# Seven products instead of eight for part of a gated unit's projections, in a two-layer decoder trunk

## The chip, the cores and the metric

The kernel runs on one core of one Trainium2 chip. The metric is the device time of one execution in microseconds (us). A core has five engines with a queue of their own each: TensorE (PE in the profile, with PEld for the loads of its stationary operand), VectorE (DVE), ScalarE (ACT), GpSimd (POOL) and SyncE (SP), which here only issues DMAs. Each engine takes its instructions in the order in which the program emits them; engines wait for each other by semaphores.

## The reference

Two decoder layers on 256 tokens of width 1024, all in float32. Each layer has four sub-layers between norms:

```python
h += 1/2 * post(SwiGLU_a(pre(h)))
h +=       post(W_out [ norm(MLA heads) ; norm(dilated-window heads) ])
h += 1/2 * post(SwiGLU_b(pre(h)))
h +=       post((p[i] W_ple) * sigmoid(pre(h) W_gate))

def swiglu(x, w_gate, w_up, w_down):
    return (jax.nn.silu(x @ w_gate) * (x @ w_up)) @ w_down
```

`x` is 256 x 1024, `w_gate` and `w_up` are 1024 x 2816 and `w_down` is 2816 x 1024. There are four such gated units (two per layer), and their weights are most of what is read and multiplied.

## The kernel before

**Precision.** A float32 number is split into two pieces of 12 significant bits, hi and lo, kept as fp32r. A product x @ w is three matmuls per block of 128 in the contracted dimension: hi.hi, hi.lo and lo.hi (`mm3`, lines 321 to 323). A matmul takes a 128 x 128 block of x, transposed, as stationary operand and up to 512 columns of w as moving operand.

**Weights.** `Weights` streams all weights in the order of use. A load on SP's queue brings a raw tile of 128 x 2048 float32 (1 MB, four buffers). `prepare()` makes one piece of 128 x 1024 out of half a raw tile: ACT copies it to hi (line 152), then DVE subtracts to get lo (line 153). Ten pairs of hi and lo are there in the gated units, eight in the attention, where the other two pairs' memory holds attention tiles (`kdt`, `grp`, `vm`, `vd`).

**A gated unit** (`ffn`) walks over six chunks of the hidden width: five of 512 columns and one of 256. The 256 tokens are two tiles, t = 0 and 1. Per chunk TensorE does gate for both tiles, up for both tiles (G0, G1, U0, U1; in a unit that follows another sub-layer the first chunk goes G0, U0, G1, U1), 24 matmuls each at 512 columns, and then down (D0, D1), also 24 each, into four PSUM banks that are kept over the whole unit. Between them ACT applies silu to gate (line 448), DVE multiplies it with up (`hm`, line 453), TensorE transposes that (`tp`, line 398), and ACT and DVE split the transpose into hi and lo (lines 401 and 402) as the stationary operand of down.

**Order.** The emission order is written out: `PLAN` lists, for each phase of matmuls, at which steps (three matmuls each) a weight piece is prepared and at which steps other work is inserted. A phase that finds a piece missing prepares it on the spot (`need`).

```python
self.nc.scalar.activation(hv, raw, AF.Copy)
self.nc.vector.tensor_tensor(lv, raw, hv.bitcast(F32), op=ALU.subtract)
...
gate(0, c, *(pend if c == 0 else []), lo_last=False)
gate(1, c)
hm0 = up(0, c)
hm1 = up(1, c, h0)
...
down(0, c, h1)
down(1, c)
```

`h0` and `h1` are the transposes and splits of the two tiles' products (`hid_t`); `pend` is what is left of the norm and the transposes of the sub-layer before.

Of the kernel before, what the change touches and what calls it, by code (L numbers as in the profile page):

```python
# [17 lines left out]
P = 128  # L18
D = 1024
# [17 lines left out]
NRAW = 4  # L37
CHUNKS = [(0, 512), (512, 512), (1024, 256), (1280, 512), (1792, 512), (2304, 512)]
# [58 lines left out]
class Weights:  # L97
# [3 lines left out]
    def __init__(self, nc, raw_pool, slots):  # L101
# [3 lines left out]
        self.shut = set()  # L105
        self.slot = {}
        self.specs = []
        self.loads = []
        self.raw = {}
        self.got = {}  # L110
        self.next = 0
        self.next_load = 0

    def add(self, keys, src, a, n):
        load = len(self.loads)
        self.loads.append((src, a * len(keys), n))
        for i, key in enumerate(keys):
            self.specs.append((key, load, i, a, n, i == len(keys) - 1))

    def load_one(self):  # L120
        i = self.next_load
        if i >= len(self.loads):
            return
        src, a, n = self.loads[i]
        raw = self.raw_pool.tile([P, 2048], F32, tag="raw", name=f"raw{i}")
        view = raw[:, : a * n].rearrange("p (a n) -> p a n", n=n)
        if i == 0:
            for j in range(0, a, a // 2):
                self.nc.sync.dma_start(view[:, j : j + a // 2], src[:, j : j + a // 2])
        else:  # L130
            self.nc.sync.dma_start(view, src)
        self.raw[i] = view
        self.next_load += 1

    def pick(self):
        return next((i for i in self.free if i not in self.shut), None)

    def can(self):
        return self.next < len(self.specs) and self.pick() is not None

    def prepare(self):
        key, load, part, a, n, last = self.specs[self.next]
        while self.next_load <= load:
            self.load_one()
        raw = self.raw[load][:, part * a : (part + 1) * a, :]
        slot = self.pick()
        self.free.remove(slot)
# [3 lines left out]
        hv, lv = (v.rearrange("p (a n) -> p a n", n=n) for v in (hi, lo))  # L151
        self.nc.scalar.activation(hv, raw, AF.Copy)  # L152
# [757 lines left out]
```

## Time and profile before

| | us |
|---|---|
| two timed runs | 1054.42, 1052.02 (median 1053.22) |
| profiled execution, first to last instruction (span) | 1052.4 |
| TensorE busy in it | 1037.1 |
| VectorE busy | 645.8 |
| ScalarE busy | 528.9 |
| GpSimd busy | 51.1 |

The profile gives for each engine its busy time, for each group of instructions their count and mean duration, and for each idle time before an instruction what ended it. Matmuls overlap in TensorE's pipeline, so the duration of one is longer than the distance from one to the next; the distance is what counts in a row of them. The profiled execution's span is 0.8 us below the median of the timed runs, and nothing else of its time is recorded, so a sum made against the span is moved by 0.8 us at the end.

### The profile page before, as it was taken

The page shows a single profiled execution, that of the slowest core. Times are in us where ns is not written, and L with a number is a line of the kernel's source. Part 1 is how long each engine was busy: PE and PEld are TensorE (multiplying, and loading weights), DVE is VectorE, ACT ScalarE, POOL GpSimd, SP SyncE. Part 2 cuts the span into 40 slices and gives each one's busy share as a digit, 9 for nine tenths or more (in the row PEclk, how much of TensorE's full clock was granted, in tenths as well). Part 3 has the DMA queues.
Part 4 walks back from the last instruction along what each step waited for, and adds up shares of the span by engine and source line. Part 5 has one row for each costly group of instructions (what it writes and reads, how often), then busy time and mean ns, then how long its engine had stood idle before and what let it go on. Part 6 is the DMA issues. An engine that isn't in the chain of part 4 may idle for free.

```text
span 1052.4 us, 13069 instructions
## 1 busy us (share of the span) xinstructions
PE 1037.1 (99%) x5168; PEld 867.0 (82%) x5168; DVE 645.8 (61%) x819; ACT 528.9 (50%) x744; POOL 51.1 (5%) x123
## 2 busy tenths in 40 slices
PE   8999999999999999999999999999999999999997
PEld 5889888878888898888878888888888888988886
DVE  4765554778677455456776545557877864555474
ACT  5544443555556444444665444445564654444463
POOL 0000000210020000000110000002000200000011
PEclk9999999999999999999999999999999999999999
DMA  8864546364227564554547645455532575545601
GB/s 321 304 227 168 193 164 211 106 222 160 82 94 272 191 213 160 201 200 160 200 160 259 212 169 200 153 163 168 180 120 82 190 275 184 198 162 172 227 21 40
DMA packets 86158, 189.02 MB, mean 180 GB/s; under 512 B 3665, under 2 KB 15313, under 8 KB 86098
## 3 DMA queue, kind: packets, MB, share of 16 engines
q1 hardware_dynamic: 86098, 188.20, 52.0%
q8 instruction: 40, 0.66, 0.2%
q14 instruction: 20, 0.16, 0.0%
HBM read 187.13 MB, written 1.05 MB: 179 GB/s over the span
## 4 chain that ended last, share of the span: by engine, by line
PE 92%; DVE 3%; ACT 2%; DMA 1%; issue 1%; POOL 0%; SPq 0%; DVEq 0%; POOLq 0%; ACTq 0%
PE acc L479 23%; PE u L323 8%; PE u L321 8%; PE u L322 8%; PE g L321 7%; PE g L323 7%; PE g L322 7%; PE tp L398 3%; PE o L706 2%; PE sc L666 1%; DVE lo L153 1%; PE gt L323 1%; PE gt L322 1%; PE gt L321 1%; PE f L321 1%; PE f L323 1%
## 5 line engine op out<-in xcount | busy, mean ns | idle before, releaser
L153 DVE TENSOR_TENSOR lo<-raw,hi 128x1024 fp32r<-128x1024 f32 (+1 forms) x338 | 405.1, 1214 | 204.2 <-ACT hi L152 194.1
L152 ACT ACTIVATE hi<-raw 128x1024 fp32r<-128x1024 f32 (+1 forms) x338 | 347.2, 1049 | 170.9 <-PE u L323 79.3
L479 PE MATMUL acc<-hi,hid 128*128 128x512 f32 x704 | 201.5, 392 | 0.0
L479 PEld LDWEIGHTS acc<-hi,hid 128*128 128x128 f32 x704 | 131.7, 188 | 27.4
L321 PE MATMUL u<-hi,xh 128*128 128x512 f32 (+1 forms) x384 | 145.3, 379 | 0.0
L323 PE MATMUL u<-hi,xl 128*128 128x512 f32 (+1 forms) x384 | 143.2, 373 | 0.0
L322 PE MATMUL u<-lo,xh 128*128 128x512 f32 (+1 forms) x384 | 143.0, 372 | 0.0
L321 PE MATMUL g<-hi,xh 128*128 128x512 f32 (+1 forms) x360 | 135.0, 375 | 2.3 <-ACT xh L401 2.3
L323 PE MATMUL g<-hi,xl 128*128 128x512 f32 (+1 forms) x360 | 134.6, 374 | 0.0
L322 PE MATMUL g<-lo,xh 128*128 128x512 f32 (+1 forms) x360 | 134.5, 374 | 0.0
L479 PE MATMUL acc<-lo,hid 128*128 128x512 f32 x352 | 118.3, 395 | 0.0
L323 PEld LDWEIGHTS u<-hi,xl 128*128 128x128 f32 x384 | 72.3, 188 | 13.0
L322 PEld LDWEIGHTS u<-lo,xh 128*128 128x128 f32 x384 | 72.4, 188 | 12.1
L321 PEld LDWEIGHTS u<-hi,xh 128*128 128x128 f32 x384 | 72.3, 188 | 12.0
L321 PEld LDWEIGHTS g<-hi,xh 128*128 128x128 f32 x360 | 68.5, 190 | 14.4 <-ACT xh L401 2.7
L322 PEld LDWEIGHTS g<-lo,xh 128*128 128x128 f32 x360 | 68.5, 190 | 12.3 <-DVE lo L153 0.5
L323 PEld LDWEIGHTS g<-hi,xl 128*128 128x128 f32 x360 | 68.4, 190 | 12.4 <-DVE xl L402 0.6
L479 PEld LDWEIGHTS acc<-lo,hid 128*128 128x128 f32 x352 | 66.2, 188 | 13.2
L401 ACT ACTIVATE hid<-tp 128x512 fp32r<-128x512 f32 (+1 forms) x48 | 27.0, 563 | 95.6 <-PE tp L398 95.6
L453 DVE SCALAR_TENSOR_TENSOR hm<-u,rs,silu 128x512 f32<-128x512 f32 (+1 forms) x48 | 33.7, 703 | 65.1 <-PE u L323 65.1
L448 ACT ACTIVATE silu<-g,rs 128x512 f32<-128x512 f32 (+1 forms) x48 | 31.3, 652 | 81.3 <-PE g L323 81.2
L402 DVE TENSOR_TENSOR hid<-tp,hid 128x512 fp32r<-128x512 f32 (+1 forms) x48 | 31.0, 647 | 44.0 <-ACT hid L401 43.6
(216 smaller groups left out, 1195.0 us busy)
## 6 DMA issues: line engine op xcount, KB each, us to landing
raw<-in_ffn_up SPq DMA_DIRECT2D x44, 1024.0 KB, 5.1
raw<-in_ffn_down SPq DMA_DIRECT2D x44, 1024.0 KB, 5.0
raw<-in_ffn_gate SPq DMA_DIRECT2D x43, 1024.0 KB, 5.2
raw<-in_w_in SPq DMA_DIRECT2D x12, 1024.0 KB, 5.2
raw<-in_w_out SPq DMA_DIRECT2D x8, 1024.0 KB, 5.1
raw<-in_w_ple_gate SPq DMA_DIRECT2D x8, 1024.0 KB, 5.1
gain<-in_norm_gains SPq DMA_DIRECT2D x15, 512.0 KB, 4.0
raw<-in_w_in SPq DMA_DIRECT2D x4, 832.0 KB, 5.2
```

The lines of the kernel that those rows point to most:

```text
L152: self.nc.scalar.activation(hv, raw, AF.Copy)
L153: self.nc.vector.tensor_tensor(lv, raw, hv.bitcast(F32), op=ALU.subtract)
L321: nc.tensor.matmul(ps, sh, wh, start=first, stop=False)
L322: nc.tensor.matmul(ps, sh, wl, start=False, stop=False)
L323: nc.tensor.matmul(ps, sl, wh, start=False, stop=last)
L398: nc.tensor.transpose(ps[:, j * P : (j + 1) * P], src[:, (b0 + j) * P : (b0 + j + 1) * P], ident)
L401: nc.scalar.activation(hv, v, AF.Copy)
L402: nc.vector.tensor_tensor(dl[:, k0 + b0 : k0 + b0 + nb, :], v, hv.bitcast(F32), op=ALU.subtract)
L448: nc.scalar.activation(s[:, :w], ps[:, :w], AF.Silu, scale=rx[t][:, 0:1])
L453: nc.vector.scalar_tensor_tensor(hm[:, :w], ps[:, :w], rx[t][:, 0:1], sg[t][:, c0 : c0 + w], op0=ALU.mult, op1=ALU.mult)
L479: nc.tensor.matmul(accs[t][n], hid[t][x][:, b, :], ws[w][:, 0, n * 512 : (n + 1) * 512], start=first and x + w == 0, stop=final and x == 1)
L706: nc.tensor.matmul(dst, pt[:, b * P : (b + 1) * P], va[:, kb, hd, :], start=kb == 0, stop=kb == t)
```

## The change

One stretch of 1024 hidden columns (two of the 512-column chunks, from column 1280 on) becomes a Strassen unit `"s"` in each of the four gated units. Gate and up are there computed as 2 x 2 blocks (token tile by half of the columns, contracted over halves of the 1024 input columns), with seven block products P1 to P7 instead of eight.

- **The sums of x.** In the first chunk, once the norm's factor is known, `scaled()` rebuilds x = hi + lo and multiplies it by that factor, which two small matmuls have spread over the partitions. `sums()` makes four combinations of x's blocks and splits them into hi and lo, in the memory that the two extra pairs had. `rescale(t)` writes the scaled x back as hi and lo, so the later chunks need no factor.
- **The sums of the weights.** For each of the two halves of a block, `prepare()` makes a piece out of the raw tile as it stands; then the raw tile gets another block added: by a DMA that adds on arrival, issued from GpSimd's queue (`then`), or, for P6, by a DVE add in front of the split (`plus`).
- **The products.** `strassen(c)` runs 12 matmuls per product and combines the results by DVE operations on PSUM and SBUF.
- **Everywhere.** Raw tiles are 128 x 1024 (0.5 MB) in eight buffers; there are eight pairs of hi and lo throughout. In the gated units `PLAN` is replaced by `flow` and `pump`: while the program is emitted, two clocks are carried along, of TensorE (0.227 us per matmul of 512 columns) and of DVE (an estimate per operation), and a piece is prepared where the DVE clock is at most 0.5 us ahead, a pair is free, the piece's due time `at` is within 5 us, and a DMA that adds to its raw tile was issued at least 8.5 us ago (`LAND`). The attention and the last sub-layer keep `PLAN`.

The diff, cut to its core (unchanged lines stand where they give the place):

```diff
-NRAW = 4
-CHUNKS = [(0, 512), (512, 512), (1024, 256), (1280, 512), (1792, 512), (2304, 512)]
+NRAW = 8
+MM = 0.227
+UNITS = [("c", 0, 512), ("c", 512, 512), ("c", 1024, 256), ("s", 1280, 1024), ("c", 2304, 512)]
+PRODUCTS = ("P1", "P5", "P6", "P3", "P2", "P7", "P4")
...
+        key, src, a, n, name, plus, then, at = self.specs[self.next]
+        load = self.load_of[name]
+        last = load if plus is None else max(load, self.load_of[plus[0]])
+        while self.next_load <= last:
+            assert self.raw_free, (key, list(self.raw))
             self.load_one()
+        raw = self.raw[load]
+        slot = self.free.pop(0)
         self.slot[key] = slot
         hi, lo = (pool.tile([P, cols], F32R, tag=tag, name=name)[:, : a * n]
                   for name, (pool, tag, cols) in zip(("hi", "lo"), self.slots[slot]))
         hv, lv = (v.rearrange("p (a n) -> p a n", n=n) for v in (hi, lo))
+        if plus is not None:
+            self.nc.vector.tensor_tensor(raw, raw, self.raw[self.load_of[plus[0]]], op=ALU.add)
+            self.dve += 1.2
         self.nc.scalar.activation(hv, raw, AF.Copy)
         self.nc.vector.tensor_tensor(lv, raw, hv.bitcast(F32), op=ALU.subtract)
+        self.dve += 1.2
         self.got[key] = (hv, lv)
         self.next += 1
+        if then is not None:
+            target, blocks = then
+            self.nc.gpsimd.dma_start(self.raw[self.load_of[target]], blocks, accum_op=ALU.add)
+            self.ready[target] = max(self.pe, self.dve) + self.LAND
+        if plus is not None:
+            self.used(self.load_of[plus[0]])
+        self.used(load)
     def tick(self):
         if self.can():
             self.prepare()
+    def pump(self, us):
+        self.pe += us
+        self.dve = max(self.dve, self.pe - 1.0)
+        while self.can() and self.dve <= self.pe + 0.5:
+            spec = self.specs[self.next]
+            if spec[7] is not None and (self.pe < spec[7] - 5.0 or self.pe < self.ready.get(spec[4], -99.0)):
+                return
+            self.prepare()
...
+                    for dt, prod, load, k, n, plus, then in (
+                        (-17.0, "P1", A, 0, 0, None, (A, block(0, 1))),
+                        (-5.0, "P5", A, 0, 0, None, None),
+                        (-2.5, "P6", A, 0, 0, (B, block(1, 1)), (A, block(1, 0))),
+                        (-1.0, "P3", B, 1, 1, None, (B, block(0, 1))),
+                        (8.5, "P2", C, 1, 0, None, None),
+                        (11.5, "P7", B, 1, 1, None, None),
+                        (14.0, "P4", A, 0, 0, None, None),
+                    ):
+                        todo.append((now + dt + 1.3 * i, dict(key=(l, f, u, name, prod, i), src=block(k, n), a=2, n=512,
+                                                              load=load, plus=plus, then=then)))
+                now += 84 * MM
+            now += 1.0
+            for j in range(8):
+                todo.append((now + 12 * MM * j - 5, dict(key=(l, f, u, "D", (j + 4) % 8), src=wd[:, f0 // P + (j + 4) % 8 : f0 // P + (j + 4) % 8 + 1],
+                                                         a=1, n=1024)))
+            now += 96 * MM + 0.9
...
+    def flow(gen, *inserts):
+        inserts = list(inserts)
+        n = 0
+        for us in gen:
+            n += 1
+            while inserts and inserts[0][0] <= n:
+                inserts.pop(0)[1]()
+            W.pump(us)
+        for _, fn in inserts:
+            fn()
     def run(gen, name, *fns):
...
+        def down_pairs(c, b0, hs):
+            for b in range(0, 4, 2):
+                for t in range(T):
+                    for j in range(b, b + 2):
+                        ws = W.need((l, f, c, "D", b0 + j))
                         for x, w in ((0, 0), (0, 1), (1, 0)):
+                            for n in range(2):
+                                down_mm(t, n, x, w, j, hs, ws, False, False)
+                        if t == 1:
+                            W.finish((l, f, c, "D", b0 + j))
+                        yield 6 * MM
...
+        def scaled():
+            rb = bank("rb")
+            dg = k2("dg")
+            for t in range(T):
+                nc.scalar.activation(dg[:, t * P : (t + 1) * P], ident, AF.Copy, scale=rx[t][:, 0:1])
+            for t in range(T):
+                nc.tensor.matmul(rb[:, t * P : (t + 1) * P], ones, dg[:, t * P : (t + 1) * P], start=True, stop=True)
+            for t in range(T):
+                xs[t] = k4("xs").rearrange("p (k q) -> p k q", q=P)
+                nc.vector.tensor_tensor(xs[t], xh[t].bitcast(F32), xl[t].bitcast(F32), op=ALU.add)
+                nc.vector.tensor_tensor(xs[t], xs[t], rb[:, None, t * P : (t + 1) * P].to_broadcast([P, KD, P]), op=ALU.mult)
+            W.dve += 4.9
+        def split_x(dh, dl, src):
+            nc.scalar.activation(dh, src, AF.Copy)
+            nc.vector.tensor_tensor(dl, src, dh.bitcast(F32), op=ALU.subtract)
+            W.dve += 0.7 * src.shape[1] / 4
+        def sums():
+            x11, x12, x21, x22 = xs[0][:, :4], xs[0][:, 4:], xs[1][:, :4], xs[1][:, 4:]
+            views = {}
+            for name, tag, cols in (("P5", "kdt", 1024), ("P6", "grp", 1024), ("P7", "vm", T * H * VW), ("P3", "vd", T * H * VW)):
+                v = work.tile([P, cols], F32R, tag=tag, name=f"s{name}")[:, :1024].rearrange("p (c k q) -> p c k q", c=2, q=P)
+                S[name] = (v[:, 0], v[:, 1])
+                views[name] = k2(f"f{name}").rearrange("p (k q) -> p k q", q=P)
+            for name, i0, i1, op in (("P5", x21, x22, ALU.subtract), ("P6", None, x11, ALU.subtract), ("P7", x11, x21, ALU.subtract),
+                                     ("P3", x12, None, ALU.add)):
+                i0 = views["P5"] if name == "P6" else i0
+                i1 = views["P6"] if name == "P3" else i1
+                nc.vector.tensor_tensor(views[name], i0, i1, op=op)
+                W.dve += 0.7
+                split_x(*S[name], views[name])
+        def rescale(t):
+            split_x(xh[t], xl[t], xs[t])
+            S.update({"P1": (xh[0][:, :4], xl[0][:, :4]), "P2": (xh[0][:, 4:], xl[0][:, 4:]), "P4": (xh[1][:, 4:], xl[1][:, 4:])})
+        def product(c, mat, name, ps, on=False):
+            sh, sl = S[name]
+            for i in range(2):
+                wh, wl = W.need((l, f, c, mat, name, i))
+                for j in range(2):
+                    k = 2 * i + j
+                    for m, (x, w) in enumerate(((sh, wh), (sh, wl), (sl, wh))):
+                        nc.tensor.matmul(ps, x[:, k, :], w[:, j, :], start=not on and k + m == 0, stop=k == 3 and m == 2,
+                                         skip_group_check=on)
+                    if j == 1:
+                        W.finish((l, f, c, mat, name, i))
+                    yield 3 * MM
...
+        def strassen(c):
+            sgs = {}
+            for mat in "GU":
+                def out(t, n, src, tmp):
+                    if mat == "G":
+                        if tmp:
+                            nc.scalar.activation(src, src, AF.Silu)
+                            sgs[t, n] = src
+                        else:
+                            sgs[t, n] = k2("sg")
+                            nc.scalar.activation(sgs[t, n], src, AF.Silu)
+                    else:
+                        dve(sgs[t, n], src, sgs[t, n], op=ALU.mult)
+                pa = bank("pa")
+                flow(product(c, mat, "P1", pa))
+                s1 = keep_copy(pa, "s1")
+                pd = bank("pd")
+                flow(product(c, mat, "P5", pd))
+                s5 = keep_copy(pd, "s5")
+                pb = bank("pb")
+                flow(product(c, mat, "P6", pb))
+                u2 = k2("u2")
+                dve(u2, pb, s1, op=ALU.add)
+                flow(product(c, mat, "P3", pd, on=True))
+                dve(s1, pd, u2, op=ALU.subtract)
+                out(0, 1, s1, True)
+                flow(product(c, mat, "P2", pa, on=True))
+                out(0, 0, pa, False)
+                pc = bank("pc")
+                up = mat == "U"
+                flow(product(c, mat, "P7", pc), *([(2, lambda: hid_t(0, sgs[0, 1], 4, hid2))] if up else []))
+                dve(u2, pc, u2, op=ALU.add)
+                dve(s5, s5, u2, op=ALU.subtract)
+                out(1, 1, s5, True)
+                pq = bank("pq")
+                flow(product(c, mat, "P4", pq), *([(2, lambda: hid_t(0, sgs[0, 0], 4))] if up else []))
+                dve(u2, pq, u2, op=ALU.add)
+                out(1, 0, u2, True)
+            hid_t(1, sgs[1, 1], 4, hid2)
+            flow(down_pairs(c, 4, hid2), (2, lambda: hid_t(1, sgs[1, 0], 4)))
...
+        for c, (kind, f0, w) in enumerate(UNITS):
             nb = w // P
+            if kind == "s":
+                hid2 = [tuple(k2(n, F32R).rearrange("p (b q) -> p b q", q=P) for n in (f"h{t}", f"l{t}")) for t in range(T)]
+                strassen(c)
+                if c == last:
+                    return post_down(c, 4, 0)
+                flow(down_pairs(c, 0, hid))
+                continue
             h0 = lambda: hid_t(0, hm0, nb)
             h1 = lambda: hid_t(1, hm1, nb)
+            if c == 0 and len(pend) == 3:
+                gate(0, c, (1, pend[0]), lo_last=True)
+                hm0 = up(0, c, (2, pend[1]), (6, pend[2]))
+                gate(1, c, (4, h0), (6, scaled))
+                hm1 = up(1, c, (1, sums), (7, lambda: rescale(0)))
+            elif c == 0:
+                gate(0, c, (7, pend[0]), (7, pend[1]))
+                gate(1, c)
+                hm0 = up(0, c, (1, scaled), (4, sums))
+                hm1 = up(1, c, (6, h0), (7, lambda: rescale(0)))
             else:
+                gate(0, c)
                 gate(1, c)
                 hm0 = up(0, c)
+                hm1 = up(1, c, (6 * w // 512, h0))
+            if c == last:
+                return post_down(c, nb, 0, h1)
             if c == 0:
                 accs.update({t: acc(f"acc{t}") for t in range(T)})
+            flow(down(0, c, nb, 0, False), (5 * nb // 4, h1), (5 * nb // 4, lambda: rescale(1) if c == 0 else None))
+            flow(down(1, c, nb, 0, False))
+            if c == 0 and len(pend) == 2:
                 setup_late()
```

`hm0` and `hm1` are emitted at the end of `up`, after everything that was inserted into it. `down` does, for each piece D of 128 hidden columns, six matmuls for its tile and is the first to call `need` for that piece.

More of the change, by code (lines that the diff above doesn't have):

```diff
@@ L120, in load_one @@
     def load_one(self):
         i = self.next_load
-        if i >= len(self.loads):
+        if i >= len(self.loads) or not self.raw_free:
             return
         src, a, n = self.loads[i]
-        raw = self.raw_pool.tile([P, 2048], F32, tag="raw", name=f"raw{i}")
+        slot = self.raw_free.pop(0)
+        raw = self.raw_pool.tile([P, 1024], F32, tag=f"raw{slot}", name=f"raw{i}", bufs=1)
         view = raw[:, : a * n].rearrange("p (a n) -> p a n", n=n)
[L127 to L131, printed above, removed]
@@ L489, in ffn, with up @@
-        last = len(CHUNKS) - 1
-        for c, (f0, w) in enumerate(CHUNKS):
-            nb = w // P
-            first = c == 0 and len(pend) == 3
-            kind = "start" if c == 0 and not first else "first" if first else "last" if c == last else "mid" if w == 512 else "small"
+        def up(t, c, *inserts):
+            w = UNITS[c][2]
+            ps = bank("u")
+            keys = [(l, f, c, "U", j) for j in range(w // 128)]
+            flow(proj(ps[:, :w], t, keys, t == 1), *inserts)
+            hm = k2("hm")
+            if c == 0:
+                nc.vector.scalar_tensor_tensor(hm[:, :w], ps[:, :w], rx[t][:, 0:1], sg[t][:, :w], op0=ALU.mult, op1=ALU.mult)
+            else:
+                nc.vector.tensor_tensor(hm[:, :w], ps[:, :w], sg[t][:, :w], op=ALU.mult)
+            W.dve += 0.7 * w / 512
+            return hm
@@ new lines, in hid_t, with down_mm, down @@
+        def hid_t(t, hm, nblk, into=None):
+            into = into or hid
+            split_t(hm, nblk, into[t][0], into[t][1])
+            W.dve += 0.65 * nblk / 4
+        def down_mm(t, n, x, w, b, hs, ws, first, final):
+            nc.tensor.matmul(accs[t][n], hs[t][x][:, b, :], ws[w][:, 0, n * 512 : (n + 1) * 512],
+                             start=first and x + w == 0, stop=final and x == 1)
+        def down(t, c, nb, b0, end, hs=None):
+            hs = hs or hid
+            halves = [[0], [1]] if end else [[0, 1]]
+            for ns in halves:
+                for b in range(nb):
+                    ws = W.need((l, f, c, "D", b0 + b))
+                    i = 0
+                    for x, w in ((0, 0), (0, 1), (1, 0)):
+                        for n in ns:
+                            down_mm(t, n, x, w, b, hs, ws, c == 0 and b == 0, end and b == nb - 1)
+                            i += 1
+                            if i % 3 == 0:
+                                if t == 1 and i == 3 * len(ns) and ns[-1] == 1:
+                                    W.finish((l, f, c, "D", b0 + b))
+                                yield 3 * MM
```

206 lines of the change are left out of this document (101 added, 105 removed).

## The prediction

> **What bounds the kernel now.** I read the page's first two parts and its chain first: which engine is full, whether evenly, and what the end hangs on.
>
> ```profile
> PE 1037.1 (99%) x5168; PEld 867.0 (82%) x5168; DVE 645.8 (61%) x819; ACT 528.9 (50%) x744; POOL 51.1 (5%) x123
> ...
> DVE  4765554778677455456776545557877864555474
> ...
> PE 92%; DVE 3%; ACT 2%; DMA 1%; issue 1%; POOL 0%; SPq 0%; DVEq 0%; POOLq 0%; ACTq 0%
> ```
>
> TensorE is on 92% of the chain. DVE is at 61% of the span, at 40 to 80% in every slice. As a busy PE may still be waiting inside, I then asked for the two chunks that the change replaces (first unit, 99.42 to 166.82 us), for the small chunk ahead of them, and for the chain in the first chunk of a later unit, where the distance of the matmuls can be read.
>
> ```profile
> core 0: us, PE busy (x) PEld busy (x) DVE busy (x) ACT busy (x) POOL busy (x), PEclk, DMA share, GB/s
> 99.42:133.12 33.70, 33.70 (x153) 27.83 (x153) 18.39 (x18) 15.81 (x18) 0.00 (x0) 1.00 0.54 188
> 133.12:166.82 33.70, 33.70 (x153) 27.81 (x152) 17.22 (x17) 14.86 (x17) 0.00 (x0) 1.00 0.54 182
> ...
> 82.00:99.42 17.42, 17.42 (x126) 16.39 (x125) 7.96 (x10) 6.79 (x9) 0.00 (x0) 1.00 0.53 182
> ```
>
> ```profile
> 335.14 3.42 PE acc L479 x15
> 338.56 0.44 PE tp L398 x4
> 339.00 7.56 PE acc L479 x33
> ```
>
> 48 matmuls in 3.42 + 7.56 us are 0.229 us each; a group of four transposes takes 0.44. A chunk's 144 matmuls at 0.229 and a little for its transposes are its 33.70 us: TensorE doesn't wait there at all. So matmuls taken away are worth their full 0.229, as long as DVE, at some 17.5 of 33.7 us in a plain chunk, keeps up. DVE's durations, and what it waits for:
>
> ```profile
> L153 DVE TENSOR_TENSOR lo<-raw,hi 128x1024 fp32r<-128x1024 f32 x326 | 393.5, 1222 | 199.1 <-ACT hi L152 189.2
> L152 ACT ACTIVATE hi<-raw 128x1024 fp32r<-128x1024 f32 x326 | 337.1, 1056 | 159.6 <-PE u L323 68.6 <-PE acc L479 59.2 <-PE g L323 22.3
> ...
> L453 DVE SCALAR_TENSOR_TENSOR hm<-u,rs,silu 128x512 f32<-128x512 f32 x40 | 29.9, 747 | 60.5 <-PE u L323 60.5
> L402 DVE TENSOR_TENSOR hid<-tp,hid 128x512 fp32r<-128x512 f32 x40 | 27.6, 691 | 32.9 <-ACT hid L401 32.6
> ...
> L401 ACT ACTIVATE hid<-tp 128x512 fp32r<-128x512 f32 x40 | 24.0, 599 | 72.6 <-PE tp L398 72.6
> ...
> L673 ACT ACTIVATE p<-sc,mx 128x128 f32<-128x128 f32 x32 | 8.7, 382 | 4.6 <-DVE mx L670 4.6
> ```
>
> ```profile
> 19.53 1.29 DVE L402 TENSOR_TENSOR xl<-tp,xh 128x512 fp32r<-128x512 f32 x2 [2.26 <-ACT xh L401]
> 23.76 8.20 DVE L153 TENSOR_TENSOR lo<-raw,hi 128x1024 fp32r<-128x1024 f32 x7 [2.94 <-ACT hi L152]
> ```
>
> Back to back a split costs DVE 8.20 / 7 = 1.17 us and an operation of 512 columns 0.65. Each split's DVE half waits for ACT's half.
>
> **The change part by part.** *Removed.* Gate and up of two chunks are 192 matmuls; 2 x 7 products of 12 are 168. 24 fewer in each of four units: 96 x 0.229 = 22.0 us, all on the path. Down's matmuls and the number of transposes stay.
>
> *The spread of the factor.* Two ACT copies of 128 x 128 (0.38 each, by L673) and two small matmuls stand in TensorE's order six steps into a phase. TensorE waits for the copies, of which some 0.5 is not covered, and does the matmuls, at most a group of transposes: 0.8 us, 3.2 for four.
>
> *DVE in the first chunk.* New are four operations of 1024 columns (`scaled`), four combinations with their splits (`sums`), and two rescales. For the three units that follow a sub-layer, with zero at the chunk's first matmul and phases of 24 x 0.229 = 5.5 us in the order G0, U0, G1, U1, D0, D1: `scaled` is emitted after six of eight steps of G1, at 15.1. From there DVE runs in order: 4 x 1.17 = 4.7; then for each combination 0.69, ACT's copy 0.60, the split 0.69 and two hand-offs of some 0.05, 8.2 together, because the split stands right behind its combination and DVE has nothing to do between; then the first rescale, whose ACT copy (1.06) overlaps the last split: 1.6; then `hm1`, emitted behind all inserts of U1: 0.75. That ends at 30.4. Of the four pieces for down, two pairs are freed in G1 ahead of `scaled`; the third piece is held back, since the DVE clock then stands at 19.9 against TensorE's 15.0 and passes 27 with `sums`. It is made by `need` behind `hm1`, ready at 31.5. D0 begins at 22.0, reaches that piece after 12 matmuls at 24.7 and its lo by 25.2. **TensorE stands 6.3 us.** The fourth piece is queued behind `h1` and the second rescale: transposes 0.44, ACT 0.60 and 1.06, DVE 1.22 and 1.17 put it 4.5 later, at 36.0, when TensorE has got to 33.3: 2.7 more. Together 9.0. In the very first unit `scaled` is a step into U0 and `sums` behind it; `hm0` waits for both, its transposes stand in U1: 5.0 us, then 3 for the first and last pieces of down: 8. Sum 3 x 9 + 8 = 35 us. Its lower bound leaves out all ACT hand-offs (12.9 in place of 16.4 us of chain): 4 x 4 = 16; its upper adds 1 us of wait to each chunk and the two PSUM-fed multiplies at 1.5: about 44.
>
> *DVE around the seven products.* The count first: 28 pieces in place of 16 (12 x 1.17 more), four weight sums of 1024 columns, 14 operations of 512 on the results in place of 4. In a weight sum's piece DVE adds, waits for ACT's 1.06, then splits: 3.5 us in one go where the DVE clock books 2.4. Eight pairs let at most four products (P1, P5, P6 and, once small chunk's down frees a pair, P3) be made ahead. From that point to the second piece of the down that follows DVE has 24 splits (28.1), two weight sums with their waits (4.5), 14 x 0.65 and 4 x 0.65 of transposed lo, 44.3 us; TensorE needs that piece after 38.4 (gate and up) and 3.0 more on either side: **at least 2.9 us too much**. Walked in order I find more. In the small chunk P5's two splits stand ahead of `hm1`, P6's 3.5 us ahead of lo of `h1`: D1 waits 3. In up, P3's pieces are made late, and P7 needs their raw tile after an adding DMA. Nothing in this trace adds on arrival; the nearest rows are 512 KB loads:
>
> ```profile
> raw<-in_ffn_gate SPq DMA_DIRECT2D x2, 512.0 KB, 7.0
> raw<-in_w_kv_up SPq DMA_DIRECT2D x2, 512.0 KB, 3.6
> ```
>
> From 3.6 to 7.0 us; I take 6, nearer to the crowded one, as such a DMA also reads its target. P7 then waits 2 to 5. P4's second half: three results (2.0), a down piece (1.17, its due time sorts before) and its own split (1.17) follow P7's end, against six matmuls (1.4), with a lo between: 3.7. The second down piece: 1.4. That is 10 to 13 us; I take **9 per unit, 36 in all**, under the walk, since a wait in one place gives DVE time for the next. Bounds 4 x 2.9 = 12 and 4 x 13 = 52. DMA bytes grow by 4 MB a unit, 16 on 189; at a DMA share of 0.54 I cost that at nothing beyond the waits above. GpSimd's other work (5%) has nothing queued there in these stretches.
>
> The Trainium skill (DMA: Bandwidth & Descriptors, "Anatomy of one DMA — SWDGE (gpsimd) path") gives 2.0 us plus bytes / 436e3 for a DMA of that queue, an estimate of 3.2 us for 512 KB. By it P7's waits would be at their lower end and the sum some 6 us smaller; no row here shows such a DMA.
>
> **The sum.** 1052.4 - 22.0 + 3.2 + 35 + 36 = 1104.6, and 0.8 for the distance of span and median: **1105 us**, 5% slower.
>
> **The rivals.** *Half absorbed, no change.* DVE's hand-offs hide and only the counted excess shows: 1052.4 - 22.0 + 3.2 + 16 + 12 + 0.8 = 1062. For it: in plain chunks DVE idles half the time, and runs ahead whenever TensorE stands. Against it: the split needs ACT's hi, and L153's idle time is 189 of 199 us that wait.
>
> *The pieces are early enough, faster.* If the third down piece of the first chunk is made before `scaled`, and the P4 pieces before the down piece, TensorE meets no missing piece; price nothing, and 1052.4 - 22.0 + 3.2 + 0.8 = 1034. It decides at 15.1 us of the chunk: a third pair must be free there and the DVE clock under TensorE's. For it: 33.70 us chunks without any wait. Against: the third pair comes free 0.6 us later.
>
> *TensorE's clock falls in the gaps, slower still.* The start of the trace shows it:
>
> ```profile
> 13.85 0.63 PE L322 MATMUL g<-lo,xh 128*128 128x512 f32 x1
> 14.27 0.63 PE L323 MATMUL g<-hi,xl 128*128 128x512 f32 x1
> ...
> 17.12 0.40 PE L322 MATMUL g<-lo,xh 128*128 128x512 f32 x1
> 17.35 0.39 PE L323 MATMUL g<-hi,xl 128*128 128x512 f32 x1
> ```
>
> 0.42 us apart until about 16.4, 0.23 after. From the first gate matmul at 10.17 that is 6.2 us at half speed, 2.9 lost. If each of eight long stalls (6.3 in the first chunks, 3.7 at P4) brought that back, 23 us more: 1128. Against it: PEclk reads 9 throughout once the kernel runs, and no mid-kernel gap is there to show it.
>
> The Trainium skill (TensorE: Matmul & The Clock Gate, "Part 1: The HAM clock gate (the "warmup" mystery)") has the clock halved after an idle window of about 3.4 us, which is this rival; the start agrees with its two rates.
>
> **How the numbers follow.** The forecast has 0.58, its own range 1075 to 1130 from the bounds above; half absorbed 0.27; early enough 0.05; the clock 0.10. The range 1048 to 1137 leaves out the early case, the lower edge of the absorbed one and the tail of the clock: under 2 in 10. 2%, about what a measurement of this kernel can tell, is 1032 to 1074. Faster 0.02: the early case with a free factor; same 0.32: 0.27, the rest of the early case and a forecast's low edge; slower 0.66.
>
> **What would show it.** 96 fewer 512-column matmuls; DVE near 80% busy; in each first chunk a TensorE gap of some 6 us in D0 released by DVE lo, with `hm1` just before; a gap before P4's second half in up; first-chunk windows of 43 us in place of 34. Wrong it would be if a third down piece is split before `scaled`, if ACT's half of the combinations doesn't hold DVE, or if adding DMAs take well over 7 us, when the products' stretch would grow beyond the range.

## The result and the profile after

The changed kernel takes 1225.32 us (median of two runs, 1223.41 and 1227.22) against 1053.22: 1.164 times the time before, 95% interval 1.158 to 1.169. The forecast was 1105 us with a range up to 1137: the direction was right, and 120 us were missing.

First the page of the changed kernel: busy times, the 40 slices, DMA queues and the landing times of the weight loads (KB each, median us from issue to landing).

```profile
PE 1098.5 (90%) x5088; PEld 882.5 (72%) x5088; DVE 786.2 (64%) x979; ACT 588.2 (48%) x840; POOL 121.0 (10%) x171
...
PE   7799959999997998699987998699999979986997
...
DVE  5645755687687556656766566457776775674584
...
PEclk9799989999998998899987998799999979996999
...
q1 hardware_dynamic: 84418, 179.82, 44.2%
q0 software_dynamic: 13056, 25.17, 11.9%
...
raw<-in_ffn_up SPq DMA_DIRECT2D x80, 512.0 KB, 5.0
raw<-in_ffn_gate POOLq DMA_DIRECT2D x24, 512.0 KB, 8.2
raw<-in_ffn_up POOLq DMA_DIRECT2D x24, 512.0 KB, 10.3
```

No engine is full from end to end: TensorE has slices at 5 to 8 tenths, and VectorE, at 64% of the span, has none at 9. The granted clock drops in the same slices in which TensorE idles. The adding DMAs, the only ones on queue q0, land 8.2 and 10.3 us after their issue, a plain load of the same size in 5.0, and they take 0.47% of the DMA engines' span per MB where plain loads take 0.25%.

Then the second gated unit by stage (first chunk; second; small; the stretch of 1024 columns; last) in the changed kernel, and the first and the fourth of these in the kernel before. Columns: window, length, busy time and count of each engine, clock, DMA share, GB/s.

```profile
356.70:405.20 48.50, 40.82 (x170) 31.54 (x169) 37.27 (x41) 26.19 (x36) 3.40 (x6) 0.86 0.45 155
405.20:438.80 33.60, 33.60 (x154) 27.83 (x153) 16.66 (x17) 15.05 (x17) 1.27 (x1) 1.00 0.54 173
438.80:459.50 20.70, 18.21 (x125) 16.17 (x124) 9.83 (x11) 6.18 (x9) 2.40 (x2) 1.00 0.54 133
459.50:548.60 89.10, 73.58 (x282) 55.64 (x281) 56.59 (x56) 41.06 (x48) 10.93 (x9) 0.89 0.77 203
548.60:583.90 35.30, 34.88 (x162) 28.56 (x161) 20.80 (x24) 17.46 (x25) 3.25 (x4) 1.00 0.52 172
```

```profile
311.20:346.40 35.20, 35.20 (x166) 28.99 (x164) 27.42 (x31) 24.47 (x31) 3.48 (x6) 1.00 0.71 247
...
397.60:465.00 67.40, 67.40 (x306) 55.66 (x305) 34.45 (x33) 29.72 (x32) 0.00 (x0) 1.00 0.55 187
```

The stretch that loses 24 matmuls grows from 67.4 to 89.1 us, the first chunk from 35.2 to 48.5, and a plain chunk stays at 33.6. The same over all four units, each stage from its first matmul to the next stage's, and for the kernels of the experiments below (us; "rest" is the span less these four columns):

| kernel | first chunks | second | small | 1024 columns | rest | span |
|---|---|---|---|---|---|---|
| before | 143.9 | 134.8 | 69.8 | 269.4 | 434.5 | 1052.4 |
| after | 209.3 | 138.3 | 81.1 | 354.4 | 442.4 | 1225.4 |
| e1 all chunks plain | 151.7 | 134.5 | 74.9 | 269.1 | 443.7 | 1073.9 |
| e9 the same, ten pairs | 145.4 | 134.5 | 74.8 | 269.1 | 454.4 | 1078.3 |
| e2 no sums of x | 154.4 | 134.5 | 83.3 | 352.8 | 440.7 | 1165.7 |
| e3 no adding DMA | 206.2 | 137.3 | 80.4 | 308.3 | 442.2 | 1174.4 |
| e4 products alone | 150.9 | 134.5 | 74.6 | 304.1 | 442.8 | 1107.0 |
| e5 and no hold | 151.6 | 134.5 | 74.6 | 280.6 | 443.6 | 1084.9 |
| e10 and P4 first | 153.4 | 134.5 | 74.6 | 277.8 | 440.9 | 1081.1 |
| e7 sums later | 157.2 | 142.7 | 81.2 | 351.3 | 442.2 | 1174.5 |
| e12 and no hold | 159.4 | 142.9 | 82.0 | 330.2 | 442.0 | 1156.5 |
| e8 first wait filled | 199.9 | 140.5 | 80.4 | 352.0 | 442.7 | 1215.6 |
| e11 products' waits filled | 206.9 | 140.5 | 81.2 | 354.7 | 443.5 | 1226.8 |

Of the 173.0 us between the spans, 85.0 lie in the products' stretch, 65.4 in the first chunks, 11.3 in the small ones, 3.5 in the second ones and 7.9 elsewhere.

The gap in the first chunk's down, in the second unit: VectorE's timeline, then TensorE's (start, duration, instruction, and in brackets the idle time before it and what ended it).

```profile
383.47 0.69 DVE L613 TENSOR_TENSOR sP<-fP,sP 128x512 fp32r<-128x512 f32 x1 [0.70 <-ACT sP L612]
384.07 0.68 DVE L627 TENSOR_TENSOR fP<-xs 128x512 f32<-128x512 f32 x1
385.45 0.69 DVE L613 TENSOR_TENSOR sP<-fP,sP 128x512 fp32r<-128x512 f32 x1 [0.70 <-ACT sP L612]
...
389.53 0.75 DVE L550 SCALAR_TENSOR_TENSOR hm<-u,rs,silu 128x512 f32<-128x512 f32 x1
390.19 1.22 DVE L178 TENSOR_TENSOR lo<-raw,hi 128x1024 fp32r<-128x1024 f32 x1
```

```profile
389.36 1.22 PE L562 MATMUL acc<-hi,hid 128*128 128x512 f32 x2 [4.74 <-ACT hi L177]
391.46 0.79 PE L562 MATMUL acc<-lo,hid 128*128 128x512 f32 x1 [0.89 <-DVE lo L178]
392.06 1.06 PE L486 MATMUL tp<-ident,hm 128*128 128x128 f32 x4
395.69 1.22 PE L562 MATMUL acc<-hi,hid 128*128 128x512 f32 x2 [1.30 <-ACT hi L177]
```

It is the forecast's picture: each combination waits 0.70 us for ScalarE's copy, `hm` and then the third down piece's lo come behind the whole chain, and TensorE stands 4.74 + 0.89 = 5.6 us, where 6.3 was forecast. But the four transposes behind the gap take 1.06 us, a row that reads 0.60 in the trace before: the clock has been halved.

In the second unit's up, ScalarE's timeline, TensorE's two longest waits in P7, and TensorE's window over P7:

```profile
505.30 1.06 ACT L177 ACTIVATE hi<-raw 128x1024 fp32r<-128x1024 f32 x1 [7.20 <-DMA raw<-in_ffn_up]
511.06 0.60 ACT L489 ACTIVATE h<-tp 128x512 fp32r<-128x512 f32 x1 [4.70 <-PE tp L486]
```

```profile
506.41 0.80 PE L643 MATMUL pc<-hi,sP 128*128 128x512 f32 x1 [4.70 <-ACT hi L177]
512.65 0.80 PE L643 MATMUL pc<-hi,sP 128*128 128x512 f32 x1 [1.63 <-ACT hi L177]
```

```profile
506.40:516.20 9.80, 7.23 (x16) 4.76 (x17) 4.27 (x4) 2.49 (x3) 0.00 (x0) 0.50 0.51 123
```

ScalarE's half of P7's first piece waits 7.2 us for an adding DMA. TensorE stands 7.3 us in P7: 4.70 and 1.63 for the two hi, 0.9 for the two lo. P7's 12 matmuls and four transposes, 3.2 us at full clock, take 9.8, of which it is busy for 7.2 at half clock.

### The profile page after: what moved, and what is told of

Read it like the earlier page. It is cut to its first block, busy times and chain, and to the rows that moved or that the text cites. A ratio compares the mean times of both kernels' runs of the same rounds, so it can differ in the third digit from the quotient of the medians.

```text
span 1225.4 us, 13837 instructions
## 1 busy us (share of the span) xinstructions
PE 1098.5 (90%) x5088; PEld 882.5 (72%) x5088; DVE 786.2 (64%) x979; ACT 588.2 (48%) x840; POOL 121.0 (10%) x171
## 3 DMA queue, kind: packets, MB, share of 16 engines
q1 hardware_dynamic: 84418, 179.82, 44.2%
q0 software_dynamic: 13056, 25.17, 11.9%
## 5 line engine op out<-in xcount | busy, mean ns | idle before, releaser
L178 DVE TENSOR_TENSOR lo<-raw,hi 128x1024 fp32r<-128x1024 f32 (+2 forms) x386 | 454.4, 1215 | 206.5 <-ACT hi L177 206.1
L177 ACT ACTIVATE hi<-raw 128x1024 fp32r<-128x1024 f32 (+2 forms) x386 | 387.0, 1046 | 116.5 <-DMA raw<-in_ffn_up 35.5
L562 PEld LDWEIGHTS acc<-hi,hid 128*128 128x128 f32 x576 | 113.0, 200 | 56.5 <-ACT hi L177 25.1
L397 PE MATMUL u<-hi,xh 128*128 128x512 f32 (+1 forms) x256 | 95.3, 372 | 0.0
L398 PE MATMUL u<-lo,xh 128*128 128x512 f32 (+1 forms) x256 | 93.5, 365 | 0.0
L399 PE MATMUL u<-hi,xl 128*128 128x512 f32 (+1 forms) x256 | 93.4, 365 | 0.0
L397 PE MATMUL g<-hi,xh 128*128 128x512 f32 (+1 forms) x232 | 86.2, 372 | 2.6 <-ACT xh L489 1.7
L398 PE MATMUL g<-lo,xh 128*128 128x512 f32 (+1 forms) x232 | 85.3, 368 | 0.8 <-DVE lo L178 0.8
L399 PE MATMUL g<-hi,xl 128*128 128x512 f32 (+1 forms) x232 | 85.2, 367 | 0.0
L184 POOL DMA_DIRECT2D raw<-in_ffn_gate x24 | 29.4, 1259 | 358.4 <-DVE lo L178 356.4
L643 PE MATMUL pc<-hi,sP 128*128 128x512 f32 x64 | 29.7, 515 | 26.2 <-ACT hi L177 26.2
## 6 DMA issues: line engine op xcount, KB each, us to landing
raw<-in_ffn_up POOLq DMA_DIRECT2D x24, 512.0 KB, 10.3
```

Of the source, the lines that this page charges most:

```text
L184: self.nc.gpsimd.dma_start(self.raw[self.load_of[target]], blocks, accum_op=ALU.add)
L397: nc.tensor.matmul(ps, sh, wh, start=first, stop=False)
L398: nc.tensor.matmul(ps, sh, wl, start=False, stop=False)
L399: nc.tensor.matmul(ps, sl, wh, start=False, stop=last)
L562: nc.tensor.matmul(accs[t][n], hs[t][x][:, b, :], ws[w][:, 0, n * 512 : (n + 1) * 512], start=first and x + w == 0, stop=final and x == 1)
L643: nc.tensor.matmul(ps, x[:, k, :], w[:, j, :], start=not on and k + m == 0, stop=k == 3 and m == 2, skip_group_check=on)
```

## The experiments

Each ratio is to runs of the kernel before on the same chip (medians 1051.94 to 1052.98 us).

**e1: the streaming alone.** All chunks plain, as before, but with the new raw tiles, eight pairs and `pump`; nothing of the products.

```diff
-UNITS = [..., ("c", 1024, 256), ("s", 1280, 1024), ("c", 2304, 512)]
+UNITS = [..., ("c", 1024, 256), ("c", 1280, 512), ("c", 1792, 512), ("c", 2304, 512)]
-gate(1, c, (4, h0), (6, scaled))
+gate(1, c, (4, h0))
...
```

> The changed kernel's streaming alone: all six chunks plain, 0.5 MB raw tiles, eight pairs, emission by the two clocks; no products, no scaled, sums or rescale. Theory A (the loss is made by what the products bring: DVE's new work in the first chunk, the adding DMAs, and TensorE's clock falling in the gaps): 1055 to 1070, the 6 us found outside the units and the 6 us of the third unit's late gate pieces staying. Rival B (eight pairs and the emission order already cost much): 1085 or more.

Measured 1075.18 us, 1.021 (1.019 to 1.024), between the two expected windows. Every middle chunk of 512 columns stands at 33.6 us, so the pieces come as well as before inside a unit. Of the 21.5 us between the spans some 16 lie at passages between sub-layers: the third unit's first chunk takes 42.0 for 35.6 us (its first gate 12.7 for 6.4), and z (the attention's first projection) and the embedding's gate 1.6 to 3.1 us more each time. Some 5 lie in the small chunks, 18.7 for 17.4 each.

**e9: two more pairs.** The pairs that the attention's tiles had lent before, given back to e1.

```diff
+slots += [((work, "kdt", 1024), (work, "grp", 1024)), ((work, "vm", T * H * VW), (work, "vd", T * H * VW))]
...
```

> All chunks plain from 0.5 MB raw tiles (no products, no sums; 1075 us with eight pairs), with two pairs of hi and lo more, borrowed from the attention's tiles as in the kernel before. Theory G (the 21 us at the passages between sub-layers, gate of unit 3 at 12.7 in place of 6.4 us, each small chunk's down 1.3 longer, z and the embedding's gate 2 longer, come from eight pairs in place of ten): 1052 to 1062 us, and unit 3's first gate back under 8 us. Rival H (they come from the smaller tiles and the order in which the clock of the source admits pieces): 1068 or more.

Measured 1080.76 us, 1.026 (1.023 to 1.028): rival H in the total. The third unit's first gate is back at 6.4 us, as theory G had it, and the first chunks at 145.4; but the embedding's first gate, with the other products that stand in it, grows to 14.0 us (9.7 before, 11.3 in e1) and z to 17.6 and 16.1 (15.0 and 15.5 in e1). The loss moves with the pieces; ten pairs don't remove it. Which of the smaller tiles and the source's clock causes it stays open.

**e2 and e3: without the sums of x; without the adding DMAs.** In e2 the products take x's own blocks as operands; in e3 the later products split the raw tile as it stands.

```diff
 # e2
-hm1 = up(1, c, (1, sums), (7, lambda: rescale(0)))
+hm1 = up(1, c)
 ...
 # e3
-self.nc.gpsimd.dma_start(self.raw[self.load_of[target]], blocks, accum_op=ALU.add)
```

> The changed kernel without scaled, sums and rescale (x is neither scaled nor combined; the products read x's blocks as they stand). Theory A: the first chunks go back from 49 to 56 us to some 35, and 65 us in four units are gone: 1160, between 1150 and 1172. Rival B (the first chunks are slow by the streaming or by the clock alone): 1195 or more.

> The changed kernel with every DMA that adds on arrival left out, all else in the same order, so the weight sums lack those blocks. Theory A (P7 and P4 wait for these DMAs, and the clock falls while they do): the products' stretch falls from 89 to some 70 us, 1150, between 1135 and 1165. Rival C (DVE's own load holds the products, the DMAs are waited for only because DVE is late): 1200 or more.

e2: 1165.65 us, 1.107 (1.103 to 1.110): 60 us less than after. The first chunks lose 54.9 of them and stand at e1's length but for 2.7; the products' stretch doesn't move. So `scaled`, `sums` and `rescale` together make the first chunks' growth beyond the streaming, all but these 2.7 us.

e3: 1180.39 us, 1.121 (1.115 to 1.126), between the two expected windows, 45 us less than after. The products' stretch falls from 354.4 to 308.3. Its windows in the second unit (gate, up, down):

```profile
444.80:464.40 19.60, 19.42 (x85) 15.67 (x84) 16.45 (x16) 13.89 (x17) 0.00 (x0) 1.00 0.44 137
464.40:496.40 32.00, 22.89 (x97) 16.95 (x97) 23.56 (x26) 14.07 (x17) 0.00 (x0) 0.99 0.38 115
496.40:520.40 24.00, 24.00 (x102) 19.37 (x101) 16.22 (x16) 12.68 (x14) 0.00 (x0) 0.94 0.77 274
```

Gate is at its seven products' length (84 x 0.229 = 19.2), so there the adding DMAs were everything. Over the four units gate gives back 18 of the 46 us. Up still takes 32.0, of which TensorE is busy 22.9, with no adding DMA left.

**e4 and e5: the products alone, with and without the hold.** The hold is `LAND`, by which a piece is kept back for 8.5 us after its raw tile's adding DMA was issued. e4 leaves out the sums of x, the weight sums and the adding DMAs, with the order, the pieces and the products kept; e5 takes away the hold as well.

```diff
 # e5, beyond e4
-    LAND = 8.5
+    LAND = -99.0
```

> Seven products with nothing around them: no scaled, sums and rescale, no adding DMA, no DVE weight sum; the 28 pieces, the combinations of the results and the order stay. If the removed matmuls are worth their 22 us and only what surrounds the products costs: 1040 to 1055. Rival C (12 more splits and 10 more operations per unit on DVE hold TensorE by themselves): 1075 or more.

> Seven products alone as in e4, but without the rule that holds a piece back for 8.5 us after its raw tile's adding DMA (there are no such DMAs here, the rule alone was left). Theory D (the hold makes P7's and P4's pieces on demand, one behind the other on ACT and DVE, and TensorE waits for each): up's P7 and P4 go from 9.2 and 8.4 us back to about 3, and four units give 1108 - 40 = 1068, between 1055 and 1080. Rival C (DVE's amount of work is what holds): 1100 or more.

e4: 1107.77 us, 1.052 (1.049 to 1.055), where rival C has it. e5: 1085.59, 1.032 (1.030 to 1.034), just above the window of theory D, so that 22 of e4's 55 us aren't VectorE's work. In e4 no DMA is added, and yet `pump` holds back P7's and P4's pieces until 8.5 us after the point at which one would have been issued. VectorE's timeline in e4's up shows it idle in the middle of the shortage:

```profile
445.59 1.22 DVE L177 TENSOR_TENSOR lo<-raw,hi 128x1024 fp32r<-128x1024 f32 x1
449.39 0.69 DVE L488 TENSOR_TENSOR l<-tp,h 128x512 fp32r<-128x512 f32 x1 [2.58 <-ACT h L487]
450.33 2.36 DVE L177 TENSOR_TENSOR lo<-raw,hi 128x1024 fp32r<-128x1024 f32 x2 [0.25 <-ACT hi L176]
```

The hold costs 22 us, or 23.5 in the four stretches, 5.9 each. P7 in up takes 8.2 to 9.2 us in e4 and 3.8 in e5; P4 takes 8.4 to 10.6 in e4 and still 8.2 to 9.0 in e5. There TensorE waits for P4's second half, in the third unit's stretch (sum, times, longest):

```profile
PE pq L643 <- DVE lo L177: 2.2, 2, 1.9
PE pq L643 <- ACT hi L176: 1.6, 1, 1.6
```

With nothing but products left, the stretch is 280.6 us, still above the plain 269.4.

**e10: P4's pieces ahead of down's.** e5 with the down pieces due half a microsecond later.

```diff
-todo.append((now + 12 * MM * j - 5, dict(key=(l, f, u, "D", (j + 4) % 8), ...
+todo.append((now + 12 * MM * j - 4.5, dict(key=(l, f, u, "D", (j + 4) % 8), ...
```

> Seven products with nothing around them (no operand sums, weight sums, adding DMAs or hold; 1085.6 us, four stretches of 70), with one number changed: the due times of the down pieces half a microsecond later, so that P4's second piece of up sorts ahead of the first of them. As predicted in the sum's step on P4's second half (a down piece of 1.17 us stands before it): P4 in up falls from 9.0 to some 6.5 us, a stretch of 67 to 69, total 1074 to 1081. Rival: P4 waits for the results of the products ahead of it on DVE in any case: 1083 to 1088.

Measured 1079.98 us, 1.025 (1.023 to 1.027), as expected in the total. P4 in up falls to 6.6 in all units, but the stretches are 67.6, 69.2, 70.5 and 70.5: what P4 gained, down gives back in the later units. The third unit, up from its second product on, then down, and what TensorE waited for in the stretch:

```profile
656.00:678.00 22.00, 19.06 (x86) 14.21 (x84) 19.78 (x23) 12.95 (x17) 0.00 (x0) 1.00 0.42 144
678.00:704.10 26.10, 25.53 (x101) 20.58 (x102) 15.72 (x15) 12.00 (x13) 0.00 (x0) 0.87 0.71 256
```

```profile
PE acc L560 <- ACT hi L176: 1.6, 1, 1.6
PE tp L484 <- DVE s L655: 0.7, 1, 0.7
PE acc L560 <- DVE lo L177: 0.6, 1, 0.6
```

VectorE is busy 19.8 of these 22.0 us (20.9 of 24.8 over the whole of up): here it comes close to being the bound, as the count of the forecast had it. The down piece that now comes second is late in its turn (1.6 + 0.6), and the clock over down is 0.87.

**e6: what a wait costs.** The kernel before, with 5 to 16 small GpSimd operations in front of the transposes of `hm` in three chunks of each unit, so that TensorE meets twelve waits and nothing else changes.

```diff
-h0 = lambda: hid_t(0, hm0, nb)
+def h0():
+    for _ in range(GAPS.get((l, f, c), 0)):
+        nc.gpsimd.tensor_scalar(hm0[:, :256], hm0[:, :256], 1.0, 0.0, op0=ALU.mult, op1=ALU.add)
+    hid_t(0, hm0, nb)
```

> The kernel before with twelve waits of different length put into TensorE's order, one in each plain middle chunk, by a chain of 5 to 16 multiplications by 1 on GpSimd ahead of the transposes of the first tile. Theory E (a wait of 3 us or more drops TensorE's clock to one half, for 3.4 us or a multiple of it, so a wait costs its own length and 1.7 to 5 us more): the clock falls behind the longer waits, and their chunks are longer by more than the wait. Rival F (it takes waits of 6 us or more, or the clock stays): every chunk is longer by its wait alone.

The waits were 2.1 to 7.0 us, 44.2 in all; the span grew by 62.9 (1117.09 us in its one run). Of the other 18.7, 15.7 lie in the stages that hold the waits (the second chunks are 14.4 us longer, the 1024 columns 45.5), nearly all of it clock: TensorE worked 29 us there at half clock. The other 3 lie elsewhere, most of them at z. The first three parts start where a wait ended (of 2.93, 2.61 and 3.10 us; two windows for the second); the last row is the wait of 6.98 itself:

```profile
70.50:73.90 3.40, 3.38 (x11) 2.85 (x12) 1.34 (x2) 2.22 (x3) 0.00 (x0) 0.54 0.42 164
...
125.80:128.40 2.60, 2.58 (x14) 2.21 (x15) 1.00 (x2) 1.89 (x3) 0.00 (x0) 1.00 0.08 33
128.40:146.00 17.60, 17.60 (x81) 14.56 (x80) 9.44 (x9) 6.98 (x8) 0.00 (x0) 1.00 0.66 221
...
437.00:440.40 3.40, 3.40 (x17) 2.90 (x18) 1.86 (x3) 2.75 (x4) 0.00 (x0) 1.00 0.00 0
...
705.20:712.20 7.00, 0.02 (x2) 0.01 (x1) 0.34 (x1) 0.00 (x0) 5.86 (x14) 0.74 0.35 140
```

After 2.93 us the clock is halved for 3.4 us (11 instructions where 17 fit), after 2.61 and 3.10 it isn't; in the longest wait it falls before the wait ends (0.74). Of the others, 2.12 and 2.58 us brought no fall, 3.09 and all six of 3.57 and more did. It isn't the length alone. The clock changes in this trace only at multiples of 3.41 us from its first change. Cut into steps at these points, every full-clock step in which TensorE was idle for 62% or more was followed by half clock (ten, the kernel's end among them), and none with 55% or less. The wait of 2.93 lay mostly in one step, the one of 3.10 in two (47% and 44% idle). Even 1.98 us at the second layer's z, not one of the twelve, brought a fall, as they lay in one step; that step and the next:

```profile
773.40:776.80 3.40, 1.29 (x6) 0.96 (x6) 2.60 (x8) 0.00 (x0) 0.50 (x1) 1.00 0.70 268
776.80:780.20 3.40, 3.40 (x12) 3.16 (x12) 2.70 (x6) 0.08 (x1) 0.00 (x0) 0.50 0.60 156
```

The Trainium skill (TensorE: Matmul & The Clock Gate, "Part 1: The HAM clock gate (the "warmup" mystery)") has an activity window of 3413 ns that runs free of the kernel. The steps here agree with that length; where the page asks for an idle window, a window idle for 62% was enough here.

**e7 and e12: a lighter order.** e7 moves the sums into the second chunk, with all of the change kept; e12 adds to that no hold and e10's due time.

```diff
-hm1 = up(1, c, (1, sums), (7, lambda: rescale(0)))
+hm1 = up(1, c, (1, lambda: rescale(0)))
...
-gate(0, c)
+gate(0, c, *([(3, sums)] if c == 1 else []))
```

> The changed kernel with sums moved from the first chunk's up into the second chunk's gate, where DVE has time. Theory A (in the first chunk TensorE stands for a DVE chain of which sums are 8 us): the first chunks lose their 5 us wait and most of the half clock behind it, 10 to 12 us each; 1180, between 1165 and 1195. Rival G (the second chunk pays it back): 1210 or more.

> All of the change, with the operand sums moved into the second chunk (1179 us), and besides without the hold after an adding DMA and with the down pieces due half a microsecond later. If the hold costs as much beside the adding DMAs as it did without them (22 us for four units): 1150 to 1165. If the arrival of the adding DMAs is what the pieces wait for, so that without a hold ACT stands before them instead: 1172 to 1190. Slower than 1053 by either.

e7: 1179.11 us, 1.121 (1.117 to 1.125): the first chunks are back at 157.2 us, and the second chunk, a plain one with VectorE at half load, takes the same sums for nothing in three units (33.6) and for 8.1 us in the first. e12: 1156.22, 1.097 (1.094 to 1.100), inside the first window: hold and due time together are worth 23 us beside the adding DMAs. As the due time alone was worth 5.6 us in e10, the hold's own share here isn't shown, but lies between some 17 and 23 if the two add up. It is the fastest form of the whole change that was run, 103 us above the kernel before.

**e8 and e11: is the clock the cost?** Matmuls whose results nothing uses, put where TensorE waits: 18 ahead of the third down piece of the first chunks in three units (e8), 42 per unit around P7 and P4 (e11).

```diff
 # e8, in down()
+if c == 0 and t == 0 and b == 2 and (l, f) != (0, 0):
+    fill = bank("fill")
+    for _ in range(18):
+        nc.tensor.matmul(fill, hs[t][0][:, 0, :], ws[0][:, 0, :512], start=True, stop=True)
 # e11, in product()
+FILL = {("G", "P7", 0): 4, ("U", "P7", 0): 14, ("U", "P7", 1): 12, ("U", "P4", 0): 12}
```

> The changed kernel with 18 more matmuls (4.1 us at full clock, into a bank that nothing reads) ahead of the third piece of the first down in three of the four units, where TensorE stands 4.7 us. Theory E (the wait's clock costs more than the wait): the half clock behind it, 13.6 us long, goes, 5 to 6 us a unit: 1225 - 17 = 1208, between 1202 and 1214, by work added. Rival F (the clock isn't the cost): 1225, or up to 1238.

> The changed kernel with 42 matmuls more per unit, whose results nothing uses, where TensorE waits in the products' stretch (4 ahead of gate's P7, in up 14 ahead of P7, 12 ahead of its second half, 12 ahead of P4; 9.6 us at full clock). Theory E (half clock, some 20 us of it in each stretch, is a cost of its own there): the stretch falls from 88.6 to 78 to 83 us, total 1183 to 1205. Rival F (the pieces and the adding DMAs set the end, as in the first chunk): the granted clock rises, the stretch stays at 87 or more, total 1216 to 1232.

e8: 1219.40 us, 1.161 (1.158 to 1.165), between the two expected windows. The second unit's down in the first chunk, after and then e8, and what TensorE waited for there in e8 (sum, times, longest):

```profile
381.70:405.20 23.50, 16.34 (x54) 11.54 (x53) 17.42 (x19) 12.18 (x14) 0.00 (x0) 0.71 0.37 129
```

```profile
378.40:401.20 22.80, 18.15 (x72) 13.63 (x71) 17.35 (x19) 12.19 (x14) 0.00 (x0) 0.93 0.39 134
```

```profile
PE acc L562 <- ACT hi L177: 2.6, 2, 1.9
PE acc L562 <- DVE lo L178: 2.1, 2, 1.4
```

The clock rises from 0.71 to 0.93 and the window shrinks by 0.7 us: TensorE, at full speed for most of it, comes to the next late piece sooner and still waits 4.7 us in that window. (Of the 9.4 us by which e8's first chunks are shorter in the table, 5.5 are the first unit's, which had no filling.) e11: 1225.92, 1.163 (1.159 to 1.167): rival F in the total. Gate and up of the second unit:

```profile
463.30:486.00 22.70, 20.93 (x90) 16.39 (x89) 15.79 (x15) 14.19 (x17) 6.12 (x5) 1.00 1.05 230
486.00:529.60 43.60, 35.44 (x135) 26.72 (x134) 24.57 (x27) 14.17 (x17) 4.81 (x4) 0.87 0.60 153
```

In gate, with four matmuls of filling, the clock stays at 1.00 and the window is 22.7 us for 26.4 after (0.1 to 1.8 less in the other units). Some 2.2 of these 3.7 us are clock, eleven matmuls of P4 that stood 0.43 us apart in after; the rest is that the adding DMAs' pieces came sooner in e11. In up the clock is 0.87 (0.85 after) and the window grows from 38.7 to 43.6; over the four units up changes by -1.1 to +4.9. The filling was fixed in length and the waits aren't, so part of it may have stood in the way. What the clock alone costs in up isn't settled by this.

## Why the prediction was wrong

**What held.** TensorE bounded the kernel before, and 96 matmuls of 512 columns are gone. The spread of the factor: G0 to U1 of the second unit take 25.1 us for 23.7, 1.3 more where 0.8 was said. The first chunk's chain, its order, the piece it makes late and the length of the first gap are as walked, and the small chunk is 2.6 to 3.2 us longer (forecast 3, of which e1 shows 1.3 to be streaming).

**The products' stretch** is the step that failed. Forecast -22 + 36 = +14 us, measured +85, though the 36 were to cover the small chunks' 3 a unit as well. Taken away one after the other, the parts add up: the adding DMAs 46.1 us (e3), the weight sums and with them the sums of x 4.2 (e4), the hold 23.5 (e5), and 33.2 that e5 still stands above 269.4 - 22.0.

*The adding DMAs* were mis-sized: "I take 6" was 8.2 and 10.3, and "P7 then waits 2 to 5" was 7.3 in the second unit, behind a wait of 7.2 in ScalarE's queue. Gate, for which no such wait was forecast, met them too. The upper bound, a plain load's 7.0 from a crowded moment, was no bound for an operation that the trace didn't have; the forecast itself names "well over 7 us" as a sign of being wrong. The estimate from the Trainium skill (DMA: Bandwidth & Descriptors, "Anatomy of one DMA — SWDGE (gpsimd) path"), 3.2 us, is further off still: the fastest of the 48 adding DMAs here took 5.6.

*The hold* stood at nothing, without a reason: the walk let P7's pieces wait for their DMA, but never for `LAND`, a line of the diff, which delays a piece even when its data is there.

*VectorE's count and order*, e5's 33.2 us, looks like the 36, but that is partly luck. The 36 also had the small chunks, P7's DMA and the weight sums in them, which e5 leaves out or which lie outside this stretch. What the walk has for e5 is P4's second half, 3.7, and the second down piece, 1.4: 5.1 a unit, 20 in all. P4's wait is as walked (1.6 + 1.9 in the third unit). The second down piece waits for nothing in that unit, and the rest is what the walk left out: half clock, 3.4 to 6.8 us of it in each stretch, and waits under 1 us in other products.

VectorE, which was to be near 80% busy, is at 64% of the second unit's stretch and of the span: it waits as well. The lower edge of the forecast's range, 1075, doesn't follow "from the bounds above": they give 1062.

**The first chunks**: 38.2 us forecast, 65.4 measured. 7.8 are streaming (e1). The other 57.6 are 16.8 in the first unit, where 8.8 were forecast, and some 13.6 in each of the others, for 9.8. In the second unit's down, 23.5 us for 11.4 before, TensorE stands 7.2 us for the two late pieces (4.74 + 0.89 + 1.30 + 0.23), less than the 9.0 of the walk. The other 4.9 go for the most part with the half clock behind the gap, which the walk had at nothing. In the first unit it is the same: TensorE stands 7.5 us (3.6 for `hm`, 3.9 for pieces) for 8 forecast, and works 15 us at half clock. Half a clock can't simply be added to the sum either: in e8, with the clock at 0.93, the same pieces set the end and 0.7 us were gained in that unit.

**The streaming** was costed at nothing but a sentence on bytes. e1 measures 21.5 us, most of it at the passages between sub-layers, to which the walk never went: it looked at the chunks that the diff touches, and `pump`, eight pairs and 0.5 MB tiles hold everywhere.

**The rival of the clock** was real and had a chance of 0.10 at 23 us. e6 shows it without anything else changed: 15.7 us over twelve waits, 1.3 on the average. "No mid-kernel gap is there to show it" was an absence of evidence, taken as evidence. Its price in the changed kernel can't be added up: TensorE's mean clock is 0.936 there over 1225.4 us, so 78 us of full-speed time weren't granted. TensorE was at work in 120 of the 158 us at half clock, which puts the price at 60 us or less, and part of what is given back turns into other waits (e8, e11).

**Where the saved 22 us went.** Seven products with every other part taken away (e10) run 8.4 us longer over four units than eight plain ones. 24 matmuls fewer make a stretch that needs VectorE for 90% of up from its second product on, and its splits, twice as dense, come behind the results that they share an engine with. In the orders that were run, the gain is turned into waits before any of the sums is paid for; whether another order would keep it stays open.

## What to carry to other kernels

Where matmuls are saved by making more operands, count the operand engine's work over the shortest phase that must be fed, and give each hold, due time and queue of the emission program a term of its own: a piece held back costs the same as a piece not there. A change in how weights stream is to be walked through every passage of the kernel, not only through the stages that the arithmetic touches. An operation that the trace doesn't have needs a wider bound than its nearest relative's worst row.

## What was not expected of the hardware

- A DMA that adds on arrival took 8.2 and 10.3 us in the median for 512 KB (5.6 to 17.2 in single cases) where a plain one took 5.0, and about twice the DMA engines' time per byte (11.9% for 25.17 MB against 44.2% for 179.82).
- In the middle of a kernel waits of 1.98 and 2.93 us were enough to halve TensorE's clock for 3.4 us, one of 3.10 wasn't: in e6 it went by the idle share of a step of 3.41 us. In the changed kernel, behind a longer stall with further holes the half clock lasted 13.7 us:

```profile
386.60:400.30 13.70, 8.53 (x20) 5.45 (x21) 10.13 (x11) 8.79 (x10) 0.00 (x0) 0.51 0.28 81
```
